# A scheduler's clock picks PSUM banks by last use and knows the scan's time; two more gate products ahead of the memory's products

## The chip, the cores and the metric

The kernel runs on one core of one Trainium2 chip. The metric is the device time of one execution in microseconds (us), the median of several runs. TensorE (PE) does matrix products into eight PSUM banks; VectorE (DVE) and ScalarE (ACT) read them out ("evacuate" them) and prepare operands; GpSimd (POOL) and SyncE (SP, which issues most DMAs) work beside them.

## The reference

One layer of a decoder trunk on 1024 tokens of width 1024, all in float32:

```python
h = rms_norm(x, norm_mix)
p = h @ w_in                                    # r,k,v,w-down,a-down,g-down | conv B,C,x | gate A | gate B
p_rw = p_rw + (token_shift(p_rw) - p_rw) * mu_shift
out_a = rwkv7_branch(r, k, v, wd, ad, gd, ...)  # recurrence over tokens, 8 heads of 64
out_b = cb * conv3(cc * cx)
merged = sigmoid(ga + bg_a) * (out_a @ w_proj_a) + sigmoid(gb + bg_b) * (out_b @ w_proj_b)
x = x + merged @ w_out_mix
x = x + memory_cross_attention(rms_norm(x, norm_xattn), rms_norm(mem, norm_mem), w_q, w_kv, w_xo)
x = x + square(relu(rms_norm(x, norm_mlp) @ w_up)) @ w_down
return rms_norm(x, norm_final)
```

The recurrence is `S_t = S_{t-1} diag(w_t) + (S_{t-1} a_t) b_t^T + v_t k_t^T`, `y_t = S_t r_t`, per head. The memory has 256 tokens, with four attention heads.

## The kernel before

Each large product splits weight and activation into a rounded high part and the remainder and adds three products of 128x512 tiles: high by high, high by low, low by high. Columns of weights ("w59" is the 60th of the list `wlist`) are loaded by SP into one of two raw buffers (`wr`), split by ACT (high, `wh`) and DVE (low, `wl`), and used for two blocks of 512 tokens (b0, b1). Products of the large matrices go into PSUM tiles with the tag g (`psg`, three banks).

The stages of PE, by the times of the profile: transposes of x into the blocks b0 and b1 (`x_stage`, to 36 us); the projections of `w_in` (the list `PROJ`: k, r, v, conv parts, gates gb0 to gb7 and ga0 to ga7), beside which the recurrence runs as side work, to 664 us; keys (`mem_k`, eight) and values (`mem_v`, two halves) of the memory, with the last four of the gates ga between them, to 733 us; then merge, attention and the MLP, to the end.

The recurrence is worked in eight windows, i0 to i7, four pairs of heads (j) by two blocks (b). For each, `wkv_prepare` forms scaled operands on DVE and small products into tiles with the tag s (`pss`, two banks), `bonus_and_values` and `wkv_invert` (a forward substitution of some 60 POOL instructions, then 32x32 products on PE) follow, and `wkv_chain` carries the state over the chunks, with tiles of the tag c (`psc`, two banks). The eighth bank has the tag y.

No queue of an engine is reordered on the chip: each engine runs its instructions in the order in which the program issues them. That order is made when the kernel is built, by a small clock, the class `Scheduler`. The main stream (the large products) and the side streams are coroutines; a side stream yields a time or a condition, and it is resumed when the clock of PE, `now()`, has reached it. The clock adds up costs per instruction (`cost`), the waits for inputs (`written`), and the wait for a buffer. For the last, `slot` guesses which earlier tile's buffer a new tile gets and when that one is done (`sch.base`). The guess only moves work in the order; the buffer is really given out by the tile framework, to a tile of the same tag, by the order in which the old tiles are released in the program. Before, the guess is the tile whose last use the clock puts earliest:

```python
old = min(q, key=lambda u: sch.end.get(u, 0.0))
```

`take_s` and `give_s` count the two `pss` banks that side streams hold.

Of the kernel before, what the change touches and what calls it, by code (L numbers as in the profile page):

```python
# [18 lines left out]
D = 1024  # L19
# [22 lines left out]
class Scheduler:  # L42
# [4 lines left out]
    def __init__(self, nc):  # L47
        self.nc = nc
        self.free = {"PE": 0.0, "DVE": 0.0, "ACT": 0.0, "POOL": 0.0, "SP": 0.0, "DMA": 0.0, "LD": 0.0}
        self.writes, self.reads, self.base, self.end = {}, {}, {}, {}  # L50
        self.side = []
        self.cold = 10
        self.mode = (128, 128)
        self.port = {"DVE": [], "POOL": []}

# [12 lines left out]
    def cost(self, eng, meth, aps):  # L68
        n = self.size(aps[0])
        part = aps[0].shape[0] < 128  # L70
        psum = any(self.key(a).startswith("ps") for a in aps)
        if eng == "ACT":
            return (0.05 if psum else 0.093) + (0.093 if len(aps) > 2 else 0.0) + n / 1200 + (0.1 if part and n > 64 else 0.0)
        if eng == "DVE":
            if meth == "reciprocal":
                return 0.18 + n * 0.0066
            if meth == "tensor_reduce":
                return 0.19 + self.size(aps[1]) * 0.00104
            if part:
                return (0.2 if meth == "scalar_tensor_tensor" else 0.17) + (0.08 if 4 < n <= 64 else 0.0) + n * 0.00104  # L80
            if meth in ("tensor_scalar", "tensor_copy") and not psum:
                return 0.12 + n * 0.00068
            return (0.13 if meth == "scalar_tensor_tensor" else 0.07) + n * 0.00104
        if eng == "POOL":
            if meth == "memset":
                return 0.05 + n * 0.0007
            if meth == "pow":
                return 0.2 + n * 0.18
            if meth == "tensor_copy":
                return 0.12 + n * 0.0033  # L90
            return 0.13 + n * (0.0011 if meth == "tensor_scalar" else 0.0022)
        return 0.06
# [65 lines left out]
    def note(self, eng, meth, outs, ins):  # L158
        deps = [self.written(a, eng) for a in ins + outs] + [self.read(a) for a in outs]
        if meth == "dma_start":  # L160
            st = max([self.free[eng], self.now() - 1.0] + deps)
            self.free[eng] = st + 0.48
            n = 4.0
            for d in outs[0].shape:
                n *= d
            self.free["DMA"] = max(self.free["DMA"], self.now() - 1.0) + n / 360e3
            end = max(self.free["DMA"], st + n / 360e3) + 2.0
        else:
            st = max([self.free[eng]] + deps)
            if eng == "PE":  # L170
                st, end = self.pe(meth, outs[0], ins, max([0.0] + deps))
            else:
                st = max(st, self.now() - 1.0)
                end = st + self.cost(eng, meth, outs + ins)
                if eng in self.port and not any(self.key(a).startswith("ps") for a in outs + ins):
                    end = self.shared(eng, st, end)
            self.free[eng] = end
        lat = 0.0 if meth == "dma_start" else 0.21
        old = self.now() - 100.0
        for a in ins:  # L180
            k, r = self.key(a), self.region(a)
            self.reads[k] = [x for x in self.reads.get(k, ()) if x[1] > old and x[0] != r] + [(r, end)]
            self.end[k] = max(self.end.get(k, 0.0), end)
        for a in outs:
            k, r = self.key(a), self.region(a)
            self.writes[k] = [x for x in self.writes.get(k, ()) if x[1] > old and x[0] != r] + [(r, end, lat, eng)]
            self.end[k] = max(self.end.get(k, 0.0), end)

    def shared(self, eng, st, end):

# [71 lines left out]
def tile_hybrid_block(  # L262
# [29 lines left out]
    FIRST = ("gmix", "ones1", "mhalf", "bd1")  # L292
    BIG = ("H", "wr", "wh", "wl", "st")
    slots = {}

    def slot(tag, t):

        q = slots.setdefault(tag, [])
        if len(q) == BUFS[tag]:
            old = min(q, key=lambda u: sch.end.get(u, 0.0))  # L300
            q.remove(old)
            sch.base[sch.key(t)] = sch.end.get(old, 0.0)
        q.append(sch.key(t))
        return t
# [6 lines left out]

    def ps(tag, shape):
        return slot(tag, pp.tile(shape, F32, tag=tag, name=nm("ps" + tag), bufs=BUFS[tag]))

    held = {"n": 8}

# [287 lines left out]
        PROJ += [("cc", i), ("cx", i), ("cb", i)]  # L604
    PROJ += [("gb", i) for i in range(8)] + [("ga", i) for i in range(8)]

    HEAD = len(PROJ) - 4
    wcols = [w_cols(win, job_off(k, i), n=32 if (k, i) == ("gd", 1) else P) for k, i in PROJ]
    wlist += wcols[:HEAD]
    for q in range(2):  # L610
        i = len(wlist)
        wlist += [w_cols(w_kv[0], n * P) for n in range(4 * q, 4 * q + 4)]
        light.update(range(i, len(wlist)))
        wlist.append(wcols[HEAD + q])
    for n in range(2):
        i = len(wlist)
        wlist += [w_wide(w_kv[0], kq * 256, D + n * 512) for kq in range(4)]
        light.update(range(i, len(wlist)))
        wlist += wcols[HEAD + 2 + n:HEAD + 3 + n]
    wlist += [w_pair(w_proj_b[0], w_proj_a[0], n * P) for n in range(KD)]  # L620
    for w in (w_out_mix, w_q, w_xo):
        wlist += [w_cols(w[0], n * P) for n in range(KD)]
# [497 lines left out]
    def lora_side(name, parts, b, dst, fin):  # L1120
        yield until(("x", 1))
        for j in range(4):
# [9 lines left out]
                zt = hold([P, 2, TB])  # L1132
            z = zt[:, j % 2]
            fin(z, o2, j)
            dma(dst[cs, blk(b)], z, (name, j, b))
            if j % 2:
                sch.spawn(stored((name, j - 1, b), (name, j, b)))
# [124 lines left out]
        yield lambda: open_s["n"] + n <= BUFS["s"]  # L1262
        open_s["n"] += n

    def give_s():
        open_s["n"] -= 1

    def c3(ap):
# [5 lines left out]
    def wkv_prepare(w):  # L1274
# [64 lines left out]
        for h in range(2):  # L1339
            for par in range(2):  # L1340
                DVE.tensor_scalar(d2[HALF[h], par:8:2], o[HALF[par], :, h], 1e-24, None, op0=ALU.max)
        give_s()
        DVE.reciprocal(d2[:], d2[:])
        w["d2"] = d2

# [6 lines left out]
        def evac_products(o, q, h):  # L1352
# [7 lines left out]
            yield pace("DVE")  # L1360
            yield until(("bs", j, b))
            DVE.tensor_tensor(QZ[H, c4, :], o[H, :, C:2 * C], rows(msk[H, C:2 * C], 4), op=ALU.mult)
            give_s()

        for q in range(2):
            yield need(T1[0], T1[1], BK) + 2 * LATE
# [15 lines left out]
        for q in range(2):  # L1382
            yield from take_s()
            o = ps("s", [P, 4, P])
            yield need(o) + LATE
            for c in range(4):
                PE.transpose(o[:, c, :], BK[:, 4 * q + c, :], ident[:])
            give_s()
            ACT.activation(BKt[:, 4 * q:4 * q + 4].rearrange("p c h k -> p c (h k)"), o[:], AF.Copy)
        w["BKt"] = BKt  # L1390
        yield until(("val", j, b))

    def bonus_and_values(w, rk_, vs_, ta_, tm_):
# [17 lines left out]
        mm(o[:], cv["bdo"][:], bs[:, 1], False, True)  # L1411
        yield max(pace("DVE"), need(o))
        DVE.tensor_tensor(sw, o[:], v, op=ALU.mult)
        give_s()
        dma(d_bv[j * P:(j + 1) * P, blk(b)], sw, ("bv", j, b))


# [7 lines left out]
        for h in range(2):  # L1425
            O = HALF[1 - h]
            for par in range(2):
                yield pace("DVE")
                DVE.tensor_copy(SV[O, par:NCH:2, h, :], o[HALF[par], :, h, :])
        give_s()  # L1430
        done.add(("val", j, b))

    def wkv_relayout(w):
# [11 lines left out]
    def wkv_invert(w):  # L1445
# [43 lines left out]
        yield max(pace("DVE"), need(o))  # L1489
        for z in hi_:  # L1490
            DVE.tensor_copy(HT[z], o[z])
        give_s()
        yield need(Lb)
        yield from take_s()
        o = ps("s", [P, NCH, 32])
# [4 lines left out]
        yield need(o)  # L1500
        for a in lo_:
            ACT.activation(XT[a, :, 32:64], o[a], AF.Copy)
        give_s()

    def wkv_chain(ws):

# [19 lines left out]
        def finish(c):  # L1526
# [3 lines left out]
            if c % 2:  # L1530
                for i, w in enumerate(ws):
                    ACT.activation(flat(w)[:, (c - 1) * C:(c + 1) * C],
                                   Y[c // 2][:, i].rearrange("p a n -> p (a n)"), AF.Copy)

        for c in range(NCH):
            last = c == NCH - 1
# [37 lines left out]
            for q in range(2):  # L1574
# [6 lines left out]
                for h, H, i, w in PART[q]:  # L1581
# [2 lines left out]
                        ACT.activation(new, o2[q][H, 2, i % 2], AF.Copy, scale=pc)  # L1584
                    else:
                        DVE.tensor_scalar(new, o2[q][H, 2, i % 2], pc, None, op0=ALU.mult)
            if last:
                yield need(*[w["SV"] for w in ws]) + 0.3
                finish(c)
# [4 lines left out]
    def wkv_out(w, a_):  # L1594
# [12 lines left out]
            mm(o[:, i, :], sq[:, i * P:(i + 1) * P], cv["bd1"][:])  # L1607
        yield need(o)
        rs = rstd_of(o[:].rearrange("p a b -> p (a b)"), 8, 1.0 / 64, LN_EPS)
        give_s()  # L1610
        rb = sq.rearrange("p (a b n) -> p a b n", a=4, b=2)
        yield need(rs)
        DVE.tensor_copy(rb, rs[:].rearrange("p (a b o) -> p a b o", a=4, o=1).to_broadcast([P, 4, 2, 64]))
# [5 lines left out]
            PE.transpose(o[:, i * P:(i + 1) * P], rb[:, i].rearrange("p a b -> p (a b)"), ident[:])  # L1619
        yield max(pace("DVE"), need(o))  # L1620
        DVE.scalar_tensor_tensor(ys, ys, vc("lnw", j), o[:], op0=ALU.mult, op1=ALU.mult)
        give_s()
        yield pace("DVE")
        DVE.scalar_tensor_tensor(ys, ys, vc("lnb", j), bv, op0=ALU.add, op1=ALU.add)
        dma(d_y[cs, blk(b)], ys, ("y", j, b))
# [32 lines left out]
    def mem_prep():  # L1658
# [5 lines left out]
        for m in range(2):  # L1664
# [13 lines left out]
            for q in range(2):  # L1678
# [6 lines left out]
                yield need(o)  # L1685
                for k in range(4):
                    gained(mh[q][:, k, ms], ml[q][:, k, ms], o[:, k], vc("nmem", 4 * q + k))
                give_s()
        drop(1)
        done.add("mem")  # L1690

# [224 lines left out]
    def att_queue():  # L1916
        yield settled(d_kt, d_vm)
        yield from att_load(0)
        for hd in range(4):
            for b in range(NB):  # L1920
# [11 lines left out]
                for m in range(2):  # L1932
                    yield need(pt[m])
                    t = sb("P", [P, 2, TB], F32R)
                    ACT.activation(t[:, 0], pt[m][:], AF.Copy)
                    DVE.tensor_tensor(t[:, 1], pt[m][:], t[:, 0].bitcast(F32), op=ALU.subtract)
                    pr.append(t)
                sch.spawn(att_out(hd, b, pr), first=True)
                if b == 0 and hd < 3:
# [220 lines left out]
    def main():  # L2160
# [10 lines left out]
        sch.spawn(merge_loads())  # L2171
        sch.spawn(gate_loads())
        yield from gemm(PROJ[:HEAD], hh, hl, proj_evac, key="h", scale="r1", pair=2)
        for q in range(4):
            for n in range(4 * q, 4 * q + 4) if q < 2 else ():
                yield from mem_k(n)
            if q > 1:
                yield from mem_v(q - 2)
            if q == 3:
                drop(4)  # L2180
            yield from gemm(PROJ[HEAD + q:HEAD + q + 1], hh, hl, proj_evac, scale="r1")
        done.add("proj")
        mgh, mgl = [], []
        for n in range(KD):
# [52 lines left out]
```

## Time and profile before

| | |
|---|---|
| median of three runs | 1776.28 us (1779.83, 1775.63, 1776.28) |
| profiled execution, its own time | 1777.75 us |
| its span in the trace | 1776.0 us |
| PE busy | 1726.2 us, 97% of the span |
| DVE, ACT, POOL busy | 1079.9, 693.2, 520.4 us |
| mean granted clock of PE | 0.989 |

The span is the traced stretch of the profiled execution, 1.75 us shorter than that execution's time. In the profile an instruction's idle time stands in brackets with what released it; "issue" there means that the profile shows no releaser. The column PEclk is the share of the full clock that PE was granted.

### The profile page before, as it was taken

The page shows a single profiled execution, that of the slowest core. Times are in us where ns is not written, and L with a number is a line of the kernel's source. Part 1 is how long each engine was busy: PE and PEld are TensorE (multiplying, and loading weights), DVE is VectorE, ACT ScalarE, POOL GpSimd, SP SyncE. Part 2 cuts the span into 40 slices and gives each one's busy share as a digit, 9 for nine tenths or more (in the row PEclk, how much of TensorE's full clock was granted, in tenths as well). Part 3 has the DMA queues.
Part 4 walks back from the last instruction along what each step waited for, and adds up shares of the span by engine and source line. Part 5 has one row for each costly group of instructions (what it writes and reads, how often), then busy time and mean ns, then how long its engine had stood idle before and what let it go on. Part 6 is the DMA issues. An engine that isn't in the chain of part 4 may idle for free. (4 is left out here: it accounts for less than half of the span.)

```text
span 1776.0 us, 26498 instructions
## 1 busy us (share of the span) xinstructions
PE 1726.2 (97%) x9818; PEld 1421.6 (80%) x9818; DVE 1079.9 (61%) x1700; ACT 693.2 (39%) x1256; POOL 520.4 (29%) x879
## 2 busy tenths in 40 slices
PE   7999999989999999999999999999999999999998
PEld 5787778778778787788888888878888888888887
DVE  4577684556763545565557665596776775555543
ACT  6624221332313563322323434454444453534532
POOL 3136658218286003001313335343323310000000
PEclk9999999999999998999999999999999999999999
DMA  6733533314543428645645667345454489655441
GB/s 215 252 120 99 154 87 86 85 40 133 158 113 117 120 84 273 213 143 202 225 148 166 204 208 253 101 136 179 148 184 149 137 272 351 247 190 190 154 131 48
DMA packets 299007, 289.18 MB, mean 163 GB/s; under 512 B 40488, under 2 KB 217758, under 8 KB 298878
## 3 DMA queue, kind: packets, MB, share of 16 engines
q1 hardware_dynamic: 297806, 286.97, 50.2%
q8 instruction: 77, 1.26, 0.3%
q10 hardware_dynamic: 1072, 0.53, 0.1%
q14 instruction: 52, 0.43, 0.1%
HBM read 193.06 MB, written 94.37 MB: 162 GB/s over the span
## 5 line engine op out<-in xcount | busy, mean ns | idle before, releaser
L256 PE MATMUL psg<-H,wh 128*128 128x512 f32 x1808 | 582.6, 401 | 4.9 <-ACT wh L256 3.5
L256 PEld LDWEIGHTS psg<-H,wh 128*128 128x128 f32 x1808 | 342.1, 191 | 77.4 <-ACT wh L256 4.4
L256 PE MATMUL psg<-P,wh 128*128 128x512 f32 (+1 forms) x1240 | 371.6, 380 | 0.8 <-DVE P L256 0.8
L256 PE MATMUL psg<-H,wl 128*128 128x512 f32 x888 | 354.7, 399 | 0.1
L256 PEld LDWEIGHTS psg<-P,wh 128*128 128x128 f32 x1240 | 228.3, 188 | 44.0 <-DVE P L256 1.2
L256 ACT ACTIVATE wh<-wr 128x1024 fp32r<-128x1024 f32 (+2 forms) x180 | 137.0, 787 | 296.0 <-PE psg L256 200.7
L256 PE MATMUL psg<-P,wl 128*128 128x512 f32 (+1 forms) x620 | 235.5, 380 | 0.0
L256 DVE TENSOR_TENSOR wl<-wr,wh 128x1024 fp32r<-128x1024 f32 (+2 forms) x171 | 166.7, 994 | 60.6 <-ACT wh L256 57.9
L256 PEld LDWEIGHTS psg<-H,wl 128*128 128x128 f32 x888 | 169.8, 191 | 35.9 <-DVE wl L256 0.9
L256 ACT ACTIVATE P<-P 128x512 fp32r<-128x512 f32 (+2 forms) x258 | 153.6, 630 | 81.5 <-DVE P L256 49.9
L256 DVE TENSOR_TENSOR P<-P,P 128x512 fp32r<-128x512 f32 (+2 forms) x221 | 155.8, 740 | 20.7 <-ACT P L256 19.2
L256 POOL TENSOR_TENSOR sm<-sm,mhalf 128x8 f32<-128x8 f32 (+3 forms) x19 | 23.3, 1232 | 464.8 <-DVE sm L256 464.8
L256 PEld LDWEIGHTS psg<-P,wl 128*128 128x128 f32 x620 | 116.6, 188 | 21.4
L256 POOL TENSOR_TENSOR ex<-ex,P 128x60 f32<-128x60 f32 (+24 forms) x248 | 95.9, 387 | 37.2 <-DMA P<-dn 21.3
L256 PE MATMUL pss<-P,wh 128*128 128x512 f32 x304 | 94.5, 390 | 1.6 <-DVE P L256 1.6
L256 POOL TENSOR_TENSOR ex<-ex 128x60 f32<-128x60 f32 (+24 forms) x248 | 90.0, 363 | 19.4
L256 DVE TENSOR_TENSOR P<-psg,P 128x512 f32<-128x512 f32 x44 | 30.3, 688 | 82.6 <-PE psg L256 68.8
L256 DVE TENSOR_TENSOR st<-psg,P 128x512 f32<-128x512 f32 x40 | 27.6, 691 | 75.6 <-PE psg L256 70.5
L256 PEld LDWEIGHTS pss<-P,wh 128*128 128x128 f32 x304 | 57.1, 188 | 14.8 <-DVE P L256 2.9
L256 PE MATMUL psc<-P,wh 128*128 128x512 f32 x216 | 66.5, 389 | 0.0
L256 ACT ACTIVATE P<-P,vec 128x512 f32<-128x512 f32 (+2 forms) x57 | 40.5, 711 | 65.6 <-DVE P L256 54.8
L256 DVE TENSOR_SCALAR P<-psc,sm 64x64 f32<-64x64 f32 x120 | 32.3, 290 | 53.8 <-ACT P L256 53.7
(684 smaller groups left out, 2772.5 us busy)
## 6 DMA issues: line engine op xcount, KB each, us to landing
P<-d_t SPq DMA_DIRECT2D x56, 512.0 KB
wr<-in_w_in_dram SPq DMA_DIRECT2D x40, 512.0 KB
d_t<-P SPq DMA_DIRECT2D x64, 256.0 KB
d_x<-P SPq DMA_DIRECT2D x48, 256.0 KB
P<-d_x SPq DMA_DIRECT2D x24, 512.0 KB
d_t<-st SPq DMA_DIRECT2D x48, 256.0 KB
d_tg<-st SPq DMA_DIRECT2D x32, 256.0 KB
wr<-in_w_kv_dram SPq DMA_DIRECT2D x16, 512.0 KB
```

Of the source, the lines that this page charges most:

```text
L256: return fn(*args, **kw)
```

## The change

Three things are changed, all of which act on the order of instructions; the instructions themselves stay the same but for three fewer on DVE and on ACT (two gate weights are split whole and the first merge weight in pieces).

1. `slot` now picks, among the tiles declared used up by the new `free(...)`, the one with the earliest last access in program order (`sch.last`, a running count); with none used up, the earliest last access of all. `free` is called where `give_s` is and for the chain's and the lora's tiles.
2. ACT instructions on less than 128 partitions cost 0.1 us more in the clock also where they have 64 elements or fewer, and DVE's scan costs 0.07 + 0.0023 n instead of 0.07 + 0.00104 n.
3. `HEAD` moves by two: ga4 and ga5 are computed ahead of the memory's products. After them come mem_k0 to 3, ga6, mem_k4 to 7, mem_v0, ga7, mem_v1. Before it was mem_k0 to 3, ga4, mem_k4 to 7, ga5, mem_v0, ga6, mem_v1, ga7.

```diff
         self.count = 0
...
-            return (0.05 if psum else 0.093) + ... + (0.1 if part and n > 64 else 0.0)
+            return (0.05 if psum else 0.093) + ... + (0.1 if part else 0.0)
...
+            if meth == "tensor_tensor_scan":
+                return 0.07 + n * 0.0023
...
+        self.count += 1
+        self.last.update((self.key(a), self.count) for a in ins + outs)
...
+    used_up = set()
     def slot(tag, t):
         q = slots.setdefault(tag, [])
         if len(q) == BUFS[tag]:
-            old = min(q, key=lambda u: sch.end.get(u, 0.0))
+            old = min([u for u in q if u in used_up] or q, key=lambda u: sch.last.get(u, sch.count + 1))
             q.remove(old)
             sch.base[sch.key(t)] = sch.end.get(old, 0.0)
...
+    def free(*tiles):
+        used_up.update(sch.key(t) for t in tiles)
...
-    HEAD = len(PROJ) - 4
+    HEAD = len(PROJ) - 2
...
-    def give_s():
+    def give_s(o):
+        free(o)
         open_s["n"] -= 1
...
         yield from gemm(PROJ[:HEAD], hh, hl, proj_evac, key="h", scale="r1", pair=2)
-        for q in range(4):
-            for n in range(4 * q, 4 * q + 4) if q < 2 else ():
+        for q in range(2):
+            for n in range(4 * q, 4 * q + 4):
                 yield from mem_k(n)
-            if q > 1:
-                yield from mem_v(q - 2)
-            if q == 3:
-                drop(4)
+            if q:
+                yield from mem_v(0)
             yield from gemm(PROJ[HEAD + q:HEAD + q + 1], hh, hl, proj_evac, scale="r1")
+        yield from mem_v(1)
+        drop(4)
```

The order of PE changes from its twentieth row up to the end of the memory's products; from the merge on (732.7 us of the profile before) PE, DVE and ACT have the same order as before. Three places show how.

DVE at the first inversion's bank (window i1, around 230 us), before. `pss_343` and `pss_349` hold products of window i2 and are read by three instructions each; `SCALAR_TENSOR_TENSOR P_342<-rst` is the scan, listed under this name, which belongs to the preparation of window i3:

```order
L256 TENSOR_TENSOR wl_345_2249<-wr_313_2011,wh_344_2248 128x1024
L256 SCALAR_TENSOR_TENSOR st_350_2270<-sh_346_2251,vec_133,st_350_2270 128x512
L256 TENSOR_TENSOR P_293_1880<-pss_343_2239,sm_321_2093 64x256
L256 TENSOR_TENSOR P_304_1966<-pss_343_2239,msk_426 64x512
L256 SCALAR_TENSOR_TENSOR P_342_2233<-rst_431,P_340_2226 128x256 x2
L256 TENSOR_TENSOR P_290_1872<-pss_343_2239,msk_426 64x256
L256 TENSOR_TENSOR P_293_1880<-pss_349_2261,sm_321_2093 64x256
```

And now, where the two product tiles are `pss_342` and `pss_343`:

```order
L261 TENSOR_TENSOR wl_345_2229<-wr_313_1999,wh_344_2228 128x1024
L261 SCALAR_TENSOR_TENSOR st_349_2246<-sh_346_2231,vec_133,st_349_2246 128x512
L261 STREAM_TRANSPOSE P_278_1717<-P_196_1181 32x8x32 x2
L261 TENSOR_TENSOR P_293_1869<-pss_342_2221,sm_320_2080 64x256
L261 TENSOR_TENSOR P_306_1959<-pss_342_2221,msk_412 64x512
L261 TENSOR_TENSOR P_290_1861<-pss_342_2221,msk_412 64x256
L261 TENSOR_TENSOR P_293_1869<-pss_343_2222,sm_320_2080 64x256
L261 TENSOR_TENSOR P_307_1960<-pss_343_2222,msk_412 64x512
L261 TENSOR_TENSOR P_290_1861<-pss_343_2222,msk_412 64x256
L261 TENSOR_TENSOR st_354_2294<-psg_347_2234,P_38_184 128x512
L261 SCALAR_TENSOR_TENSOR P_341_2210<-rst_417,P_339_2203 128x256 x2
```

The three reads of the first tile now stand together; the scan has moved behind both tiles' reads.

PE there, before. The inversion has two sets of 32x32 products; the first stands far ahead of this part. Shown are the last products of window i2 into the two tiles, main products, and the second set (`pss_352`), which gets the bank of `pss_343`:

```order
L256 MATMUL pss_343_2239<-P_304_1966,P_306_1968 128x128
L256 MATMUL pss_349_2261<-P_305_1967,P_306_1968 128x128
L256 MATMUL psg_347_2254<-H_15_161,wh_325_2122 128x512
L256 MATMUL psg_347_2254<-H_23_169,wh_325_2122 128x512
L256 MATMUL psg_347_2254<-H_15_161,wl_326_2123 128x512
L256 MATMUL psg_347_2254<-H_16_162,wh_325_2122 128x512
L256 MATMUL psg_347_2254<-H_24_170,wh_325_2122 128x512
L256 MATMUL psg_347_2254<-H_16_162,wl_326_2123 128x512
L256 MATMUL pss_352_2287<-P_196_1180,P_262_1645 32x32 x16
L256 MATMUL psg_347_2254<-H_17_163,wh_325_2122 128x512
```

And now, the end of the main products behind the same products of window i2 (their last row stands ten rows ahead of this part) and the first set of the inversion (`pss_350`), which gets the bank of `pss_342`; the second follows sixteen rows later:

```order
L261 MATMUL psg_347_2234<-H_20_166,wh_321_2094 128x512
L261 MATMUL psg_347_2234<-H_28_174,wh_321_2094 128x512
L261 MATMUL psg_347_2234<-H_20_166,wl_322_2095 128x512
L261 MATMUL psg_347_2234<-H_21_167,wh_321_2094 128x512
L261 MATMUL psg_347_2234<-H_29_175,wh_321_2094 128x512
L261 MATMUL psg_347_2234<-H_21_167,wl_322_2095 128x512
L261 MATMUL psg_355_2296<-H_14_160,wh_321_2094 128x512
L261 MATMUL pss_350_2270<-P_278_1717,P_199_1189 32x32 x16
L261 MATMUL psg_355_2296<-H_22_168,wh_321_2094 128x512
L261 MATMUL psg_355_2296<-H_14_160,wl_322_2095 128x512
```

Six main products stood between the tiles' last products and the set that takes the bank of the first; sixteen stand there now.

SP at the weights of the memory, before: `in_w_kv` with 8x128 is a column of keys, with 2x512 a quarter of a half of the values, `in_w_in` a gate; the others are loads and stores of the side streams:

```order
L256 DMA wr_797_6545<-in_w_kv_dram 128x8x128
L256 DMA d_tg_146<-st_793_6506 128x512
L256 DMA d_kt_158<-st_800_6564 128x256
L256 DMA wr_804_6608<-in_w_in_dram 128x8x128
L256 DMA wr_812_6697<-in_w_kv_dram 128x2x512
L256 DMA d_kt_158<-st_810_6676 128x256
L256 DMA wr_821_6800<-in_w_kv_dram 128x2x512
L256 DMA d_kt_158<-st_817_6772 128x256
L256 DMA wr_828_6882<-in_w_kv_dram 128x2x512
```

And now the stretch that follows ga6's load:

```order
L261 DMA wr_806_6628<-in_w_kv_dram 128x8x128
L261 DMA d_tg_146<-st_810_6688 128x512
L261 DMA wr_822_6861<-in_w_kv_dram 128x8x128
L261 DMA P_471_3411<-d_bv_149 128x512
L261 DMA P_564_4356<-d_bv_149 128x512
L261 DMA P_593_4568<-d_bv_149 128x512
L261 DMA P_641_4927<-d_bv_149 128x512
L261 DMA d_tg_146<-st_820_6842 128x512
L261 DMA wr_840_6954<-in_w_kv_dram 128x2x512
L261 DMA d_kt_158<-st_835_6936 128x256
L261 DMA wr_845_7001<-in_w_kv_dram 128x2x512
```

The load of a gate between the last key and the first value is gone: keys 4 to 7 and the first half of the values follow one another.

More of the change, by code (lines that the diff above doesn't have):

```diff
@@ L49, in __init__ @@
         self.free = {"PE": 0.0, "DVE": 0.0, "ACT": 0.0, "POOL": 0.0, "SP": 0.0, "DMA": 0.0, "LD": 0.0}
-        self.writes, self.reads, self.base, self.end = {}, {}, {}, {}
+        self.writes, self.reads, self.base, self.end, self.last = {}, {}, {}, {}, {}
         self.side = []
         self.cold = 10
+        self.count = 0
         self.mode = (128, 128)
@@ L72, in cost @@
         if eng == "ACT":
-            return (0.05 if psum else 0.093) + (0.093 if len(aps) > 2 else 0.0) + n / 1200 + (0.1 if part and n > 64 else 0.0)
+            return (0.05 if psum else 0.093) + (0.093 if len(aps) > 2 else 0.0) + n / 1200 + (0.1 if part else 0.0)
         if eng == "DVE":
@@ L612, in tile_hybrid_block @@
         wlist += [w_cols(w_kv[0], n * P) for n in range(4 * q, 4 * q + 4)]
+        if q:
+            wlist += [w_wide(w_kv[0], kq * 256, D) for kq in range(4)]
         light.update(range(i, len(wlist)))
         wlist.append(wcols[HEAD + q])
[L615 to L619, printed above, removed]
+    i = len(wlist)
+    wlist += [w_wide(w_kv[0], kq * 256, D + 512) for kq in range(4)]
+    light.update(range(i, len(wlist)))
     wlist += [w_pair(w_proj_b[0], w_proj_a[0], n * P) for n in range(KD)]
@@ L1134, in lora_side @@
             fin(z, o2, j)
+            free(o2)
             dma(dst[cs, blk(b)], z, (name, j, b))
@@ L1341, in wkv_prepare @@
                 DVE.tensor_scalar(d2[HALF[h], par:8:2], o[HALF[par], :, h], 1e-24, None, op0=ALU.max)
-        give_s()
+        give_s(o)
         DVE.reciprocal(d2[:], d2[:])
@@ L1362, in evac_products @@
             DVE.tensor_tensor(QZ[H, c4, :], o[H, :, C:2 * C], rows(msk[H, C:2 * C], 4), op=ALU.mult)
-            give_s()
+            give_s(o)
         for q in range(2):
@@ L1387, in wkv_prepare @@
                 PE.transpose(o[:, c, :], BK[:, 4 * q + c, :], ident[:])
-            give_s()
             ACT.activation(BKt[:, 4 * q:4 * q + 4].rearrange("p c h k -> p c (h k)"), o[:], AF.Copy)
+            give_s(o)
         w["BKt"] = BKt
@@ L1413, in bonus_and_values @@
         DVE.tensor_tensor(sw, o[:], v, op=ALU.mult)
-        give_s()
+        give_s(o)
         dma(d_bv[j * P:(j + 1) * P, blk(b)], sw, ("bv", j, b))
@@ L1429, in bonus_and_values @@
                 DVE.tensor_copy(SV[O, par:NCH:2, h, :], o[HALF[par], :, h, :])
-        give_s()
+        give_s(o)
         done.add(("val", j, b))
@@ L1491, in wkv_invert @@
             DVE.tensor_copy(HT[z], o[z])
-        give_s()
+        give_s(o)
         yield need(Lb)
@@ L1502, in wkv_invert @@
             ACT.activation(XT[a, :, 32:64], o[a], AF.Copy)
-        give_s()
+        give_s(o)
     def wkv_chain(ws):
@@ L1533, in finish @@
                                    Y[c // 2][:, i].rearrange("p a n -> p (a n)"), AF.Copy)
+                free(Y[c // 2])
         for c in range(NCH):
@@ L1586, in wkv_chain @@
                         DVE.tensor_scalar(new, o2[q][H, 2, i % 2], pc, None, op0=ALU.mult)
+            free(*o2)
             if last:
@@ L1609, in wkv_out @@
         rs = rstd_of(o[:].rearrange("p a b -> p (a b)"), 8, 1.0 / 64, LN_EPS)
-        give_s()
+        give_s(o)
         rb = sq.rearrange("p (a b n) -> p a b n", a=4, b=2)
@@ L1621, in wkv_out @@
         DVE.scalar_tensor_tensor(ys, ys, vc("lnw", j), o[:], op0=ALU.mult, op1=ALU.mult)
-        give_s()
+        give_s(o)
         yield pace("DVE")
@@ L1687, in mem_prep @@
                     gained(mh[q][:, k, ms], ml[q][:, k, ms], o[:, k], vc("nmem", 4 * q + k))
-                give_s()
+                give_s(o)
         drop(1)
@@ L1936, in att_queue @@
                     DVE.tensor_tensor(t[:, 1], pt[m][:], t[:, 0].bitcast(F32), op=ALU.subtract)
+                    free(pt[m])
                     pr.append(t)
@@ L2173, in main @@
         yield from gemm(PROJ[:HEAD], hh, hl, proj_evac, key="h", scale="r1", pair=2)
-        for q in range(4):
-            for n in range(4 * q, 4 * q + 4) if q < 2 else ():
+        for q in range(2):
+            for n in range(4 * q, 4 * q + 4):
                 yield from mem_k(n)
-            if q > 1:
-                yield from mem_v(q - 2)
-            if q == 3:
-                drop(4)
+            if q:
+                yield from mem_v(0)
             yield from gemm(PROJ[HEAD + q:HEAD + q + 1], hh, hl, proj_evac, scale="r1")
+        yield from mem_v(1)
+        drop(4)
         done.add("proj")
```

## The prediction

> **What bounds the kernel now.** I read the page first, then the waits of PE by stretch, the timeline of PE and DVE around the long waits, and a table of windows for the granted clock. The page says that PE bounds:
>
> ```profile
> PE 1726.2 (97%) x9818; PEld 1421.6 (80%) x9818; DVE 1079.9 (61%) x1700; ACT 693.2 (39%) x1256; POOL 520.4 (29%) x879
> ```
>
> PE is idle for 1776.0 - 1726.2 = 49.8 us, so an order that changes nothing else can win only from these and from time at a lower clock. Most lies where the recurrence runs beside the projections. The first table has PE's waits for the recurrence's tiles from 140 to 520 us (total, times, longest). The second is one row of the windows view, the start from 22 to 51 us, with its width, the busy times of PE, PEld, DVE, ACT and POOL, and PEclk, the granted clock: PE is idle for 29.00 - 23.96 = 5.0 us there. The third and fourth are again waits, from 51 to 140 us and from 680 to 735 us:
>
> ```profile
> PE pss L256 <- DVE P L256: 8.2, 6, 2.6
> PE pss L256 <- issue: 3.8, 2, 2.4
> PE pss L256 <- DVE sm L256: 0.7, 1, 0.7
> PE psc L256 <- ACT P L256: 0.6, 2, 0.4
> PE pss L256 <- ACT P L256: 0.6, 2, 0.4
> ```
> ```profile
> 22.00:51.00 29.00, 23.96 (x112) 18.80 (x111) 17.65 (x30) 20.68 (x39) 9.98 (x35) 0.88 0.60 200
> ```
> ```profile
> PE psc L256 <- ACT P L256: 0.7, 2, 0.4
> ```
> ```profile
> PE psg L256 <- ACT wh L256: 3.5, 2, 2.7
> PE psg L256 <- DVE wl L256: 1.0, 2, 0.7
> ```
>
> Two long waits, with DVE's rows around the first, show what kind they are:
>
> ```profile
> 231.35 0.40 PE L256 MATMUL psg<-H,wl 128*128 128x512 f32 x1
> 234.11 0.79 PE L256 MATMUL pss<-P,P 32*32 32x32 f32 x32 [2.36 <-issue]
> 218.64 0.71 PE L256 MATMUL pss<-P,bdo 128*128 128x512 f32 x2 [1.75 <-DVE P L256]
> ```
> ```profile
> 230.47 0.75 DVE L256 SCALAR_TENSOR_TENSOR st<-sh,vec,st 128x512 f32<-128x512 f32 x1
> 231.14 0.41 DVE L256 TENSOR_TENSOR P<-pss,sm 64x256 f32<-64x256 f32 x1
> 231.58 0.69 DVE L256 TENSOR_TENSOR P<-pss,msk 64x512 f32<-64x512 f32 x1
> 232.29 1.27 DVE L256 TENSOR_TENSOR_SCAN P<-rst,P 128x256 f32<-128x256 f32 x2
> 233.59 0.42 DVE L256 TENSOR_TENSOR P<-pss,msk 64x256 f32<-64x256 f32 x1
> ```
>
> The inversion's products start at 234.11, right when the third read of the old tile (`P<-pss,msk` of 64x256) has ended at 234.01. They wait for the PSUM bank, not for data, and the scan of another window stands in the middle of the reads. I followed the waits of the pss tiles from 152 to 510 us in the same way: eleven of them, 13.4 us together, end with the old tile's last read.
>
> The longer ones also cost clock. Windows that begin where the granted clock falls, behind four of the waits, and last one around the wait at 218.64 (PEclk is the third number from the end):
>
> ```profile
> 235.50:238.91 3.41, 3.41 (x10) 2.56 (x9) 2.62 (x5) 1.34 (x3) 2.33 (x4) 0.50 0.43 116
> 368.62:372.03 3.41, 3.41 (x21) 2.39 (x21) 1.04 (x2) 0.00 (x0) 0.00 (x0) 0.50 0.20 77
> 467.61:471.02 3.41, 3.41 (x9) 2.64 (x8) 2.06 (x5) 2.26 (x4) 2.31 (x6) 0.50 0.00 0
> 494.91:498.32 3.41, 3.41 (x17) 2.71 (x14) 2.70 (x5) 0.00 (x0) 2.94 (x7) 0.50 0.32 125
> 216.50:222.00 5.50, 3.75 (x17) 2.81 (x16) 4.81 (x10) 0.05 (x1) 0.02 (x1) 1.00 0.61 191
> ```
>
> After the waits at 234, 368, 466 and 494 (and 384) PE runs for 3.41 us at half clock, which loses half of it, 1.7 us; after the one at 218 it does not.
>
> Here a rule bears on the sum. The Trainium skill, TensorE: Matmul & The Clock Gate, section "HAM oscillation — how this bites in real kernels", gives it as "no PE-idle gaps >~3.4µs". By it the waits of 2.4 us and less would cost no clock, and the forecast below would be 8.5 us higher, 1768.5; the trace agrees on the half rate and on the 3.41 us, but not on the length of the gap.
>
> **The change part by part.** Three edits reorder; none makes an instruction cheaper. Each cost is therefore a wait that goes or comes.
>
> The order of bank use, and the scan's time. *Waits that go:* at the first inversion sixteen main products now stand between the tiles' last products and the set that takes the bank, where six stood. The pace is
>
> ```profile
> 589.95 0.62 PE L256 MATMUL psg<-H,wh 128*128 128x512 f32 x2
> 590.63 0.62 PE L256 MATMUL psg<-H,wh 128*128 128x512 f32 x2
> ```
>
> three (one row between left out) in 0.68 us, 0.227 each, so 3.6 us where 1.4 were. DVE's three reads (0.41 + 0.69 + 0.42 = 1.5 us by the rows above) now stand together, the scan (1.27) behind. So 2.36 us goes with its half-clock window. At the bonus of 218.64 the distance hardly changes; the weight split that stood among the reads goes ahead of them:
>
> ```profile
> 215.32 1.22 DVE L256 TENSOR_TENSOR wl<-wr,wh 128x1024 fp32r<-128x1024 f32 x1
> ```
>
> which is most of the 1.75. The other nine I compared in the same way, distance in PE's order against the reads in DVE's: each either gets 3.6 us or more or takes another bank. I count all 13.4 us as going, then take back 3 for new waits: at the places where distance and reads are within 0.5 us of each other (six that I found), half a microsecond each. Five half-clock windows go with them: 5 x 1.7 = 8.5.
>
> *The lora's waits* (psc <- ACT P, 0.6 above, and 0.7 from 51 to 140 us) go as the distance grows there: 1.3.
>
> *The start.* The transposes of x's second block come thirteen main products later, 3 us, but DVE now has other evacuations ahead of theirs, so the 5.0 us of the second table partly move to the first products of b1. Between all gone (5.0, and of the half clock 0.12 x 29 = 3.5 by the row's PEclk: gain 8.5) and as much again (loss 8.5) I take almost nothing, a gain of 0.5, since as many evacuations stand ahead of a wait after as before.
>
> *The path through POOL.* The last inversion now waits for DVE:
>
> ```profile
> 575.81 0.22 POOL L256 TENSOR_TENSOR ex<-ex 128x8 f32<-128x8 f32 x1
> 593.13 0.35 DVE L256 SCALAR_TENSOR_TENSOR P<-pss,vec,P 128x128 fp32r<-128x128 f32 x1 [0.43 <-ACT P L256]
> 593.39 0.89 DVE L256 STREAM_TRANSPOSE P<-P 32x256 f32<-32x256 f32 x2
> 593.87 0.24 PE L256 MATMUL pss<-P,P 32*32 32x32 f32 x2 [1.49 <-DVE P L256]
> ```
>
> POOL was done at 576, 17 us ahead of the transposes; its result's transfers had landed by about 585, so some 8 us were slack, and the transposes stood on DVE behind the memory's evacuations (`P<-pss,vec,P`). In the new order 214 main products stand between the last-but-two inversion and this one, where 241 stood: 27 x 0.227 = 6.1 us less, and PE no longer loses the 6 us of waits and half clock in between. That eats the 8 us of slack by about 4. Bounds: no wait, or 8 us. I take 2 us more than now and a half-clock window in every second case: -2.9.
>
> *Costs of the two clock edits by themselves:* ACT's 0.1 and the scan's time change no instruction, and the scan hides under PE as long as it stands behind the reads.
>
> The gates ahead of the memory. Two gates' weights are light no longer, split whole; the work is the same. What changes is how the memory's weights are supplied. Two raw buffers, and the splits of consecutive values' quarters stand 4.2 us apart:
>
> ```profile
> 684.71 1.14 ACT L256 ACTIVATE wh<-wr 128x512 fp32r<-128x512 f32 x2
> 688.93 1.15 ACT L256 ACTIVATE wh<-wr 128x512 fp32r<-128x512 f32 x2 [2.56 <-DMA wr<-in_w_kv_dram]
> 695.97 0.95 PE L256 MATMUL psg<-H,wh 128*128 128x512 f32 x2 [2.68 <-ACT wh L256]
> ```
>
> PE uses up a light weight in twelve products, 2.7 us, and a gate (48 products) in 10.9. A gate lets the loads catch up. Before the change a gate follows every four light weights; after it eight light ones stand in a row. Each of the four more may be 4.2 - 2.7 = 1.5 us short: 0 to 6 us. Against that the wait for ga6 (2.68, with a half-clock window, 1.7) goes or halves. I take a loss of 1.5 net. On SP the keys' loads now queue behind more loads of `d_bv` (the order above), part of the same 1.5. The merge's loads follow on the same queue; no wait for them stands in the fourth table, and I cost them at nothing; if that slack goes, the first merge product is late next.
>
> **Sum:** 13.4 + 8.5 + 1.3 + 0.5 - 3 - 2.9 - 1.5 = 16.3 us. The profiled execution took 1777.75, 1.5 above the median of the runs; 1777.75 - 16.3 = 1761.4, and by the median 1760.
>
> **The rivals.** *The reads stay slow (slower).* The old latencies from a tile's last product to its last read were often 9 to 12 us, since DVE's work for the next window stands among the reads. At the fourth window's:
>
> ```profile
> 488.11 0.42 DVE L256 COPY P<-pss 64x256 f32<-64x256 f32 x1
> ...
> 493.89 0.43 DVE L256 COPY P<-pss 64x256 f32<-64x256 f32 x1
> 494.46 1.21 PE L256 MATMUL pss<-P,P 64*128 64x128 f32 x11 [1.58 <-DVE P L256]
> ```
>
> the four copies take from 488.11 to 494.32. In the new order five places have only 3.7 to 6.8 us between the two tiles. If the copies were as spread there, they would be short by 3.9, 4.4, 5.7, 5.4 and 5.7 us, 25.1 with 8.5 of half clock: the 23.2 gained turn into -10.4, 1787. It decides once more than two thirds of this comes. Against it: in the new DVE order the spread work mostly stands elsewhere; at the window of 5.7 the rows ahead of the last copy add up to 5.65 against 6.75. Chance 5%.
>
> *The change does not do what it says (same).* The real bank goes by release in the program, and the clock's guess of its end is still the clock's. If as many waits come back elsewhere, gains of 0 to 5: 1771 to 1776. For it: the same clock failed in eleven places. Chance 9%.
>
> *The inversion becomes the bound.* The last wait takes the whole 8 us and a window: 6.8 us more than in the sum, 1767. Chance 8%.
>
> *The half clock stays.* PE falls to half clock also with no long wait ahead, while it runs 128x2 products:
>
> ```profile
> 665.10 1.84 PE L256 MATMUL pss<-bd,P 128*128 128x2 f32 x16
> 668.99:675.82 6.83, 6.83 (x25) 5.75 (x25) 3.03 (x6) 0.72 (x1) 3.94 (x3) 0.50 0.30 114
> ```
>
> Should the small products have this effect wherever they stand, 8.5 is lost from the sum: 1768.5. Chance 8%; the Trainium skill's rule above gives the same number.
>
> **How the numbers follow.** The forecast, 70%, has a range of 1751 (nothing taken back: 23.2 + 2) to 1766. The two middle rivals end at 1767 and 1768.5, still faster. Runs of this kernel differ by some 0.3%, 5.3 us: faster is below 1771. Faster 0.70 + 0.08 + 0.08 = 0.86, same 0.09, slower 0.05. The range 1751 to 1771 leaves out the same and slower cases and the forecast's own tails.
>
> **What would show it.** In the profile after, the waits `pss <- DVE P` and `pss <- issue` from 140 to 520 us should be under 5 us, with at most one half-clock window; the inversion of the last window should wait 2 to 4 us near 575 to 585; and the waits for `wh` and `wl` among the memory's products should be 4 to 8 us. From the merge on nothing should change. I am wrong if the pss waits stay over 10 us, or if the memory's stretch takes more than 6 us longer.

## The result, and the profile after

The changed kernel takes 1753.8 us (median of four runs, 1753.05 to 1754.07) against 1775.95 us before in the same comparison: a ratio of 0.9872, 95% interval 0.9852 to 0.9891, 22 us less. The profiled execution took 1754.07 us, its span is 1752.3 us. The forecast was 1760, in a range of 1751 to 1771. The page's first line of engines, and PE's waits from 140 to 520 us, where the pss rows added up to 13.7 us before:

```profile
PE 1712.8 (98%) x9818; PEld 1413.1 (81%) x9818; DVE 1080.6 (62%) x1697; ACT 695.1 (40%) x1253; POOL 523.9 (30%) x879
```
```profile
PE pss L261 <- DVE P L261: 2.4, 4, 1.2
PE psc L261 <- DVE P L261: 0.8, 3, 0.4
PE psc L261 <- ACT s L261: 0.5, 1, 0.5
PE pss L261 <- DVE sm L261: 0.4, 1, 0.4
PE pss L261 <- PE psg L261: 0.2, 1, 0.2
```

The pss waits are 3.0 us now. PE's busy time fell too, by 13.4 us, although it does the same products; part of that is the clock. The windows view from the end of k0 to the end of window i6's inversion, the last but one (below "inversion i6"), of before and then of after (width, busy times of PE, PEld, DVE, ACT and POOL, PEclk, then the DMA engines' share and GB/s):

```profile
50.74:564.99 514.25, 498.17 (x3443) 403.64 (x3443) 324.72 (x571) 158.03 (x294) 265.90 (x650) 0.98 0.41 119
```
```profile
49.88:551.28 501.40, 496.79 (x3493) 404.62 (x3492) 325.14 (x574) 161.10 (x297) 263.47 (x643) 1.00 0.43 123
```

PE's idle time there falls from 16.1 to 4.6 us and the granted clock goes from 0.98 to 1.00: all five half-clock windows are gone. (The two stretches hold a different number of main products, about 50 more after, so their widths don't compare.)

To compare by stage, I took for each PE instruction the time to the next one's start, less what an instruction of its shape takes where nothing is waited for (0.227 us for 128x512). The sum of this excess is the time lost in a stage, to waits and to the clock alike. Its level depends on what the small products are allowed (with the median spacing of each shape the second row is 33.0 and 9.0), the gain hardly. Keys of the memory stand in the stages around the second chain too: PE's first key product comes at 595.5 us before and at 598.7 after, not at 664 as the list of stages has it.

| stage of PE | before | after | forecast gain | measured gain |
|---|---|---|---|---|
| start, to the end of k0 | 17.2 | 16.6 | 0.5 | 0.7 |
| to inversion i6 | 50.9 | 26.9 | 20.2 | 24.0 |
| last inversion, to the second chain | 3.9 | 1.1 | -2.9 | 2.8 |
| the second chain | 10.0 | 9.8 | 0 | 0.2 |
| end of the second chain to the merge (the memory's stretch) | 11.2 | 13.6 | -1.5 | -2.4 |
| merge to end, order unchanged | 12.5 | 14.1 | 0 | -1.6 |
| sum | 105.7 | 82.0 | 16.3 | 23.7 |

The last inversion, which was forecast to wait, no longer does. POOL's last instruction for it, and the two sets of its products (bracketless rows: no idle time before them):

```profile
560.45 0.22 POOL L261 TENSOR_TENSOR ex<-ex 128x8 f32<-128x8 f32 x1
576.14 0.69 PE L261 MATMUL pss<-P,P 32*32 32x32 f32 x32
579.03 0.69 PE L261 MATMUL pss<-P,P 32*32 32x32 f32 x32
```

From 600 to 720 us, the memory's products and the second chain, PE waits for `wl` and `wh` for 6.9 us. In the memory's stretch these waits stand at another place than before, at the first half of the values and at ga7, with half-clock windows at 673.97 and 684.21:

```profile
PE psg L261 <- DVE wl L261: 5.2, 4, 1.9
PE psg L261 <- ACT wh L261: 1.7, 2, 1.0
```
```profile
670.56 0.49 PE L261 MATMUL psg<-wh,P 128*128 128x512 f32 x1 [0.73 <-ACT wh L261]
672.93 0.50 PE L261 MATMUL psg<-wl,P 128*128 128x512 f32 x1 [1.87 <-DVE wl L261]
```

### The profile page after: what moved, and what is told of

The parts are those of the page before. It is cut to its first block, busy times and chain, and to the rows that moved or that the text cites. A ratio compares the mean times of both kernels' runs of the same rounds, so it can differ in the third digit from the quotient of the medians.

```text
span 1752.3 us, 26500 instructions
## 1 busy us (share of the span) xinstructions
PE 1712.8 (98%) x9818; PEld 1413.1 (81%) x9818; DVE 1080.6 (62%) x1697; ACT 695.1 (40%) x1253; POOL 523.9 (30%) x879
## 3 DMA queue, kind: packets, MB, share of 16 engines
q1 hardware_dynamic: 297806, 286.97, 50.9%
## 5 line engine op out<-in xcount | busy, mean ns | idle before, releaser
L261 PE MATMUL psg<-H,wh 128*128 128x512 f32 x1808 | 574.2, 397 | 9.5 <-ACT H L261 4.5
L261 PEld LDWEIGHTS psg<-H,wh 128*128 128x128 f32 x1808 | 337.5, 189 | 83.0 <-ACT H L261 6.2
L261 PE MATMUL psg<-H,wl 128*128 128x512 f32 x888 | 350.9, 395 | 1.8 <-DVE wl L261 1.8
L261 DVE TENSOR_TENSOR P<-P,P 128x512 fp32r<-128x512 f32 (+2 forms) x221 | 159.6, 758 | 22.3 <-ACT P L261 20.9
L261 POOL TENSOR_TENSOR ex<-ex,P 128x60 f32<-128x60 f32 (+24 forms) x248 | 92.2, 372 | 58.4 <-DMA P<-dn 42.7
L261 POOL TENSOR_TENSOR ex<-ex 128x60 f32<-128x60 f32 (+24 forms) x248 | 94.9, 383 | 19.4
L261 ACT ACTIVATE P<-psc,sm 64x64 f32<-64x64 f32 (+1 forms) x128 | 39.3, 330 | 54.1 <-DVE P L261 28.8
```

Source lines behind the costliest of these rows:

```text
L261: return fn(*args, **kw)
```

## The experiments

Theory A is the prediction's: the guess of the bank makes the pss waits, and the gates cost at the memory. Theory B, the rival: any other order scatters the waits by chance, so each part would do about as well. Theory C: the two gates are cover for the last inversion. Six runs take the three edits (bank, times of the clock, gates) alone and in pairs; the last row is the changed kernel once more, from the last group of runs below. Each row is against the kernel before on the same chip.

| bank | times | gates | median us | before, us | ratio, 95% interval |
|---|---|---|---|---|---|
| x | | | 1757.5 | 1775.4 | 0.9894 (0.9867 to 0.9922) |
| | x | | 1790.5 | 1775.4 | 1.0083 (1.0052 to 1.0114) |
| | | x | 1777.4 | 1775.4 | 1.0015 (0.9998 to 1.0032) |
| x | x | | 1763.5 | 1775.4 | 0.9942 (0.9915 to 0.9970) |
| x | | x | 1751.8 | 1775.2 | 0.9859 (0.9833 to 0.9884) |
| | x | x | 1789.1 | 1775.2 | 1.0069 (1.0043 to 1.0094) |
| x | x | x | 1755.4 | 1777.2 | 0.9879 (0.9859 to 0.9899) |

**The bank's choice alone.** The kernel before with `last`, `count`, `used_up` and `free`, and

```diff
-            old = min(q, key=lambda u: sch.end.get(u, 0.0))
+            old = min([u for u in q if u in used_up] or q, key=lambda u: sch.last.get(u, sch.count + 1))
```

> Only the choice of the bank by last use, with the list of used-up tiles; the clock's costs and the place of the gates are those of before. Theory A (the guess of the bank made the waits for the pss tiles): PE's pss waits from 140 to 520 us fall from 13.7 to under 6 us, at most one half-clock window among them, time 1755 to 1762. Theory B (any other order of the side work would have done as well, the waits are scattered by chance): pss waits of 5 to 14 us at other places, time 1762 to 1780.

1757.5 us. Its waits from 140 to 520 us:

```profile
PE pss L259 <- DVE P L259: 1.2, 2, 0.6
PE pss L259 <- issue: 0.9, 1, 0.9
PE psc L259 <- DVE P L259: 0.8, 3, 0.4
```

2.1 us of pss waits and no half-clock window there. Theory A holds: this edit alone ends the waits. It has two parts, the list of used-up tiles and the earliest last access in place of the earliest end, and no run takes them apart or counts how often the new guess names the bank that is really given out.

**The clock's times alone.**

```diff
-            return (0.05 if psum else 0.093) + ... + (0.1 if part and n > 64 else 0.0)
+            return (0.05 if psum else 0.093) + ... + (0.1 if part else 0.0)
+            if meth == "tensor_tensor_scan":
+                return 0.07 + n * 0.0023
```

> Only the clock's times for the scan and for ACT's small instructions. Theory A: the waits for the bank stay, pss waits of 10 us or more, at least three half-clock windows, time 1770 to 1778. Theory B: as much scattered as with the bank's order, 1760 to 1780 with the waits at other places.

1790.5 us, slower than either theory said. The pss waits of the same stretch grew, from 13.3 us in these four rows before to 20.0:

```profile
PE pss L258 <- DVE P L258: 9.5, 6, 2.8
PE pss L258 <- issue: 6.5, 3, 3.7
PE pss L258 <- ACT P L258: 2.0, 1, 2.0
PE pss L258 <- DVE sm L258: 2.0, 1, 2.0
```

The bank's waits stay without the bank's edit, as A says; that they grow was in neither theory. That moving work under a wrong guess can lose as well as win is an argument; no run shows where the loss comes from.

**The gates alone.**

```diff
-    HEAD = len(PROJ) - 4
+    HEAD = len(PROJ) - 2
```

> Only the two gates ahead of the memory's products. Theory A with the prediction's step on the memory: nothing changes up to 520 us, pss waits 13.7 as before, the memory's stretch loses 1.5 to 5 us, time 1776 to 1782. Theory C (the two gates are cover for the last inversions): the wait of the last inversion, 1.5 us, goes and nothing takes its place, so that the loss at the memory is about paid back, 1773 to 1778.

1777.4 us, in both ranges. The wait of the last inversion did not go; the row for 520 to 600 us:

```profile
PE pss L256 <- DVE P L256: 1.7, 2, 1.5
```

So before the bank's edit that wait was not for want of cover. C is not shown here, and it needed the next run.

**All but the gates.** The changed kernel with `HEAD` and the loops of before.

> The whole change but for the gates, which stay between the memory's products as before. Theory A: as the changed kernel up to 520 us, and without its waits for wl and wh among the memory's products (6.9 us and two half-clock windows there), so 1748 to 1752. Theory C: the last inversion then waits for its data, 3 to 8 us with a half-clock window, so 1753 to 1762, not faster than the changed kernel.

1763.5 us, 8 to 10 us slower than the changed kernel, as C says, and 1.5 us over C's range. The waits from 520 to 600 us, and the last inversion:

```profile
PE pss L261 <- DVE P L261: 4.1, 3, 3.3
PE psc L261 <- DVE P L261: 3.1, 4, 1.4
PE pss L261 <- ACT P L261: 2.1, 1, 2.1
```
```profile
570.76 0.24 PE L261 MATMUL pss<-P,P 32*32 32x32 f32 x2 [3.31 <-DVE P L261]
```

Without the two gates PE comes to the inversion's products at 567.45 and waits 3.3 us; the excess of the stage is 9.1 us (1.1 with the gates) and that of the second chain 13.0 (9.8). The memory's stretch is 8.6 instead of 13.6. The gates win 11 us and lose 5, the 5 mostly as clock: the brackets of the stretch add up to 4.4 us without the gates and 5.6 with them, but PE runs for 3.41 us at half clock without them and for 13.65 with them. In the kernel before there was little to win.

**The bank and the gates, old times.**

> The choice of the bank and the two gates, with the clock's old times. Up to the sixth inversion as the kernel with the bank's choice alone; the two gates then cover the last inversion and the chain as in the changed kernel, and the memory's stretch costs as there. Theory D (the effects add by stage): the clock's times are worth nothing here, 1749 to 1756, within 5 us of the changed kernel. Theory E (the scan's time is needed for the bank's choice): new pss waits before 520 us, over 5 us, and 1757 to 1765.

1751.8 us: theory D. The excess to inversion i6 is 23.7 us against 26.9 in the changed kernel. Theory E falls by DVE's rows at the bank of window i1's inversion:

```profile
225.60 0.42 DVE L259 TENSOR_TENSOR P<-pss,sm 64x256 f32<-64x256 f32 x1
226.04 1.12 DVE L259 TENSOR_TENSOR P<-pss,msk 64x512 f32<-64x512 f32 x2
...
229.42 2.30 DVE L259 TENSOR_TENSOR_SCAN P<-rst,P 128x256 f32<-128x256 f32 x2
```

The scan stands behind all reads though the clock has its old time. It was moved by the bank's choice.

**The times and the gates, old bank.**

> The clock's times and the two gates, with the old choice of the bank. Theory D: the waits of the kernel with the clock's times alone up to 520 us (pss waits of some 20 us), less some 8 us at the last inversion and the chain, so 1778 to 1786, slower than before. Theory B (any order does): below 1772.

1789.1 us, 3 us over D's range. The excess to inversion i6 is 59.1 us, at the last inversion 1.2, and at the memory's products 18.1: the gates end the inversion's wait here too, and what they win goes at the memory, more than I expected.

**One gate ahead instead of two.**

```diff
-    HEAD = len(PROJ) - 2
+    HEAD = len(PROJ) - 3
```

with one gate after keys 0 to 3, one after keys 4 to 7 and one after the first half of the values.

> The changed kernel with one gate ahead of the memory's products instead of two: keys 0 to 3, ga5, keys 4 to 7, ga6, values' first half, ga7, second half, so that no more than four light weights stand in a row. If the run of eight light weights made the waits for wl and wh (6.9 us and two half-clock windows from 600 to 707 us), they fall to under 4 us, and if one gate is cover enough for the last inversion, no wait of over 1 us from 520 to 600 us: 1746 to 1750. If one gate is too little: a wait of 1 to 3 us for the last inversion, 1752 to 1757. If the waits for wl and wh come from the load of DVE and ACT and not from the run of light weights, they stay: 1752 to 1756.

1762.2 us (0.9918, 0.9892 to 0.9943), slower than any of the three cases. One gate is too little: the stage of the last inversion loses 4.3 us and the second chain 15.3 (1.1 and 9.8 in the changed kernel). The waits from 600 to 720 us:

```profile
PE psg L261 <- DVE wl L261: 4.3, 6, 1.6
PE psg L261 <- ACT wh L261: 3.0, 4, 1.3
```

They stay at 7.3 us, which was the sign of the third case, the load of DVE and ACT. But they are ten short waits and no half-clock window follows them, so the memory's stretch loses 10.6 instead of 13.6 us. Not all of these 3 us belong to the run of eight light weights: the half-clock window behind the 128x2 products, at 649.80, is 3.41 us long here and 6.83 in the changed kernel (at 650.08), which is 1.7 us by itself.

**The same with the old times.**

> As the last one, with the clock's old times: the choice of the bank and one gate ahead. By theory D the sum of both gains, 1744 to 1750; by theory E 1755 or more.

1752.5 us (0.9865, 0.9835 to 0.9894), above D's range by 2.5. With the old times the waits for `wl` and `wh` from 600 to 720 us do fall with one gate less ahead, from 5.0 to 2.2. The memory's stretch is down to 6.2 us (9.8 with two gates), and the second chain takes it back, 15.0 against 11.4.

**The two times apart, and the pair again on one chip.** Four kernels beside the same runs of before (1777.2): bank, gates and ACT's time; bank, gates and the scan's time; the changed kernel; bank and gates alone.

> The changed kernel without the scan's new time in the clock (bank, gates and ACT's small instructions changed). Theory F (the clock's new times are worth nothing once the bank is chosen by last use): 1750 to 1756, within 3 us of the changed kernel. Theory E (the scan's time moved the scan behind the reads): the scan stands between the reads of the first inversion's bank again, a wait of over 1 us and a half-clock window there, 1756 or more.

> The changed kernel without ACT's new time (bank, gates and scan changed). Its order on PE differs from the changed kernel only from the chain of the first block on. Theory F: 1750 to 1756. If ACT's new time is what makes the changed kernel 2 us slower than the one without both times: 1749 to 1752, as that one.

> The changed kernel beside the others on one chip: 1752 to 1755.

> The choice of the bank and the gates, without the clock's new times, beside the changed kernel on one chip. Theory F: within 3 us of it, either way. If the new times cost something in themselves: 2 us or more faster than the changed kernel in every pair of runs, 1749 to 1752.

1754.5, 1752.6, 1755.4 and 1750.9 us (ratios 0.9873, 0.9860, 0.9879 and 0.9848, each with about 0.002 either way). In the first of them, too, DVE's scan, at 228.49, stands behind the reads of both tiles, the last at 226.73 (two rows together 1.12 us), against theory E. The changed kernel is 0.4 us over its range. Theory F's 3 us do not hold for the last, which was 4.6 us ahead of it. But the intervals overlap, so that the last is the fastest is likely and not shown: these edits were 2.0 us ahead of the changed kernel's first runs and 4.6 here, with single runs from 1746.6 to 1754.5 against 1753.1 to 1759.7. What is shown is that the clock's new times bring no gain beside the bank's choice and the gates. Kernels within 5 us of each other can hardly be told apart by one profile: from the merge on the order of PE is the same in all of them, and that part alone lost between 11.9 and 19.6 us in the twelve experiments' profiles.

## Why the prediction was right, and where it was off

The direction and the main mechanism were right. *The bank's waits:* 13.4 less 3 were to go; the pss rows fell from 13.7 to 3.0, and the run with that edit alone shows the cause. The place at 218.64, of which most was to go with the weight split, kept more than half of its 1.75 us; the split is gone from among the reads there, other work of DVE is not:

```profile
215.54 0.71 PE L261 MATMUL pss<-P,bdo 128*128 128x512 f32 x2 [1.17 <-DVE P L261]
```

*The half clock:* 8.5 us in five windows, all gone; the rival that it stays falls in this stretch. *The lora and the start:* 1.3 and 0.5 forecast; the lora's rows are gone, and the start gained 0.7. That the start agrees is in part luck: PE is idle for 29.00 - 23.62 = 5.4 us there, where it was 5.0, and the gain is a half-clock window of 3.41 us in place of one of 6.83, which the forecast did not have.

```profile
22.00:51.00 29.00, 23.62 (x112) 18.28 (x111) 18.52 (x31) 20.97 (x38) 10.73 (x35) 0.94 0.64 215
```

The sum was 16.3 and the profile gained 23.7 (the medians 22). Three terms were mis-sized.

*The path through POOL* was forecast at -2.9 and measured at +2.8, the largest miss. The step that failed is the wait, not the slack. By the trace's semaphore updates, which mark the end of a transfer, the transfers of POOL's result had landed by 584.07 us before and by 570.44 after, and PE came to the products at 593.87 and at 576.14: 9.8 us of slack became 5.7, so 4.1 went, as the prediction had it. But it then took a longer wait, between none and 8 us, although by its own count some 4 us of slack were left. The wait of 1.5 us in the profile before did not come from missing slack at all; the transposes stood right behind the memory's evacuations on DVE (593.13 and 593.39 in the prediction's rows). Now those evacuations are done at 567.2, and the transposes have 3 us to spare before PE comes:

```profile
566.82 0.35 DVE L261 SCALAR_TENSOR_TENSOR P<-pss,vec,P 128x128 fp32r<-128x128 f32 x1 [0.44 <-ACT P L261]
...
572.33 0.89 DVE L261 STREAM_TRANSPOSE P<-P 32x256 f32<-32x256 f32 x2
```

I also set the gates' effect on this path to nothing; the run without them shows that they are what keeps it free, worth 8.0 us there and 3.2 in the chain.

*The waits' size.* To inversion i6 24.0 us went, not 20.2. PE's idle time there fell by 11.5 us, where 10.4 and the lora's 1.3 were forecast, and the half clock by what was forecast, so the 3.8 us more lie elsewhere. A bracket understates a wait: the row at 365.10 of the profile before

```profile
365.10 0.40 PE L256 MATMUL psg<-H,wh 128*128 128x512 f32 x1
368.06 0.70 PE L256 MATMUL pss<-P,bdo 128*128 128x512 f32 x2 [2.56 <-DVE P L256]
```

ends at 365.50 by its modelled end, and 2.56 is counted from there; without a wait the next would have started 0.227 us after 365.10, so the loss is 2.73. (At 2.56 us it is also the longest wait, so not all of them are "2.4 us and less", as the prediction has it.) Over this stretch's 22 waits some 4 to 5 us lay beyond the brackets, by what the small products are allowed, and in the 13 after 2.3. That is about 2 of the 3.8 us. The rest is spread over instructions without a bracket, and its cause stays open.

*The memory's products* were forecast at -1.5 and lost 2.4. The mechanism, loads that do not catch up, accounts for two of the four waits there, 1.7 of 5.4 us. ACT's splits behind the waits at 670.56 (0.73 us) and at ga7 (0.99 us, at 681.04) begin at 669.88 and 680.58, when the trace's last updates of their loads, issued at 664.30 and 673.54, are 0.1 and 0.4 us old (669.77 and 680.22). The two longer waits, 1.87 us at 672.93 and 1.76 at 683.54, are of another kind, which the prediction did not have. The low part's split stands on DVE behind a product of the side work that waits for ACT, while the high part is already there:

```profile
671.58 0.69 DVE L261 TENSOR_TENSOR P<-P,P 128x512 fp32r<-128x512 f32 x1 [2.19 <-ACT P L261]
672.19 1.29 DVE L261 TENSOR_TENSOR wl<-wr,wh 128x512 fp32r<-128x512 f32 x2
...
682.46 0.69 DVE L261 TENSOR_TENSOR P<-P,P 128x512 fp32r<-128x512 f32 x1 [4.83 <-ACT P L261]
683.07 1.09 DVE L261 TENSOR_TENSOR wl<-wr,wh 128x256 fp32r<-128x256 f32 x3
```

Nor is a cost of the run of light weights shown in general. The two gates made this stretch lose 0.8 us more in the kernel before, 9.2 more beside the new times, and 5.0 more in the changed kernel, but 2.1 less beside the bank's choice with the old times. No run changes the order of DVE there alone.

One cause was wrong: I gave the scan's move to the clock's new time. The run with the bank and the gates alone shows the scan behind the reads without it, and the times alone made the kernel 15 us slower. Why the clock orders worse with these times stays open; no run here separates it further than that each of the two times, beside the bank and the gates, changes little.

Of the rivals, "the change does not do what it says" fell with the first run, and "the reads stay slow" with the 3.0 us. "The inversion becomes the bound" came true only in kernels with fewer gates ahead.

## What to carry to other kernels

Where a scheduler models which buffer a new tile gets, look at that guess before the instruction times: the choice by last use won 18 us here, and new times under the old choice lost 15. Before a filler is moved, look at which waits would follow if the present ones went: the gates were worth nothing without the bank's edit and 8 to 10 us in the changed kernel; with the bank's edit and the old times they were worth 6, with intervals that overlap. And count a wait from the usual start of the next instruction, not from the end that the bracket starts at.

## What the runs showed of the clock

The granted clock changes only on a fixed grid of 3.413 us, in all fourteen profiles: in the one before the windows of half clock begin at 235.50, 368.62, 385.69 and 467.61, which lie 39, 5 and 24 steps apart. What goes with a change is how busy PE was in the grid's last step. Here are six such steps, each with PE's busy time in it behind the width (the first three are from the profile before, the others from after, where 673.97 is the step that followed 670.56):

```profile
365.21:368.62 3.41, 0.85 (x5) 0.51 (x4) 2.60 (x8) 0.82 (x3) 0.00 (x0) 1.00 0.00 0
215.02:218.43 3.41, 1.86 (x9) 1.21 (x7) 3.32 (x5) 0.27 (x1) 0.00 (x0) 1.00 0.38 105
464.20:467.61 3.41, 1.98 (x38) 1.44 (x37) 3.33 (x7) 0.22 (x1) 0.00 (x0) 1.00 0.00 0
```
```profile
667.14:670.56 3.42, 2.69 (x13) 1.88 (x12) 2.25 (x4) 1.23 (x3) 0.00 (x0) 1.00 0.93 304
670.56:673.97 3.41, 1.54 (x6) 1.05 (x7) 1.90 (x3) 1.40 (x3) 0.00 (x0) 1.00 0.98 364
673.97:677.38 3.41, 3.41 (x10) 2.63 (x9) 2.35 (x4) 1.89 (x4) 0.00 (x0) 0.50 1.03 404
646.66:650.08 3.42, 3.42 (x32) 3.42 (x32) 0.93 (x4) 2.54 (x7) 2.46 (x2) 1.00 0.75 230
```

PE was busy for 25% of the step at 365.21, for 45% at 670.56 and for 58% at 464.20, and half clock followed (at 368.62, 673.97 and 467.61); for 55% at 215.02 and 79% at 667.14, and it did not. Over all fourteen profiles, steps at full clock from 20 to 1740 us: under 45% busy, half clock followed in 38 of 38; from 45 to 65% in 26 of 84; from 65 to 95% in none of 341. What decides between 45 and 65% stays open. So the wait of 1.43 us at 466.57 cost 1.7 us of clock and the one of 1.75 at 218.64 none, and two short waits in one step count together: in the run with the times alone, 0.73 and 1.00 us of idle time in the step at 21.52 (49% busy) were followed by half clock at 24.93.

The exception is the last row: PE is busy throughout, with 128x2 products among the others, and half clock followed, as in 11 of some 6,500 full steps. All eleven hold 16 to 24 such products; of the 27 full steps with 16 or more, 11 were followed by half clock, and all 7 with 20 or more. Against the Trainium skill, TensorE: Matmul & The Clock Gate, section "HAM oscillation — how this bites in real kernels", with its idle gap of about 3.4 us, the measurement decides: idle time of more than 55% of one step, 1.9 us of 3.41, was always enough.
